# Rolling a matrix along its rows: 512 of 8192 rows taken through SBUF whole

## The chip, the cores and the metric

One Trainium2 chip, one core. The time is device microseconds (us) of one execution, less is better. MB are millions of bytes, GB/s billions of bytes a second.

## The reference

```python
def setup_inputs():
    return {
        "x": np.random.randn(8192, 8192).astype(np.float32),
        "shift": 100,
    }

def reference(x: np.ndarray, shift: int) -> np.ndarray:
    return np.roll(x, shift, axis=1)
```

Each row of 8192 float32 values (32,768 bytes) is rotated by 100 places: `out[r, 100:]` is `x[r, :8092]`, and `out[r, :100]` is `x[r, 8092:]`. Nothing is computed; the kernel only moves 268.44 MB from one place in HBM (the chip's main memory) to another.

## The kernel before

With a shift `s` of 100, the kernel sets `a` to 256 and `g = a - s` to 156. Every output row is cut at column 256.

**The bodies, columns 256 to 8191, are copied from HBM to HBM** (L33 to L43). A block is 64 rows, and each block is four transfers of 16 rows that lie four rows apart; each of the 16 DMA engines gets one row, 7,936 values or 31,744 bytes, of each transfer. The engines SP and ACT issue them in turn, each on its own DMA queue. The last 4 of the 128 blocks have their columns split in two, so that the last transfers are half as long. Each queue issues 248 whole and 16 half transfers and waits for nothing but room in its queue.

**The heads, columns 0 to 255, go through SBUF** (L55 to L80; the core's on-chip memory of 128 partitions), and GpSimd (POOL) issues all their transfers, on a third queue, its ring. They are cut in 16 stages of 512 rows, four rows to a partition (`Q = 4`). A stage has three loads: L72 loads 256 values that straddle a row's end and the next row's start into `t`, for three of the four rows; L73 loads the last 100 values of the fourth row into `h`; L76 loads the first 156 values of the first row into `h`. VectorE (DVE) copies the two parts of `t` to their places in `h` (L74, L77). L80 stores `h`, 256 values for each of 512 rows. The pools `reads` and `heads` have 16 buffers each, one for every stage, so no load waits for a store. In program order GpSimd issues all 48 loads and then the 16 stores. The program uses eight semaphores in turn for GpSimd's transfers, so each transfer is issued only when the one eight places before it has landed.

`single_packet=True` on the heads' transfers asks for few packets. A DMA engine serves its queues by packets, and the trace records each packet with its queue, its bytes, its start and its duration; every transfer also ends with a packet of 4 bytes on each engine that tells its completion.

Of the kernel before, what the change touches and what calls it, by code (L numbers as in the profile page):

```python
# [1 line left out]

# [4 lines left out]


@with_exitstack
def kernel(  # L10
    ctx: ExitStack,
    tc: tile.TileContext,
    x: bass.AP,
    shift: int,
    out: bass.AP,
):
    nc = tc.nc
    n_rows, n_cols = x.shape
    s = shift % n_cols
    a = -(-s // 128) * 128  # L20
    if 0 < a <= 384 and a + 128 <= n_cols:
        a += 128
    g = a - s
    P = nc.NUM_PARTITIONS
    engines = [nc.sync, nc.scalar]
    n_chunks = 16
    rows = n_rows // n_chunks

    xm = x.rearrange("(c e j) w -> c j e w", e=16, j=4)
    om = out.rearrange("(c e j) w -> c j e w", e=16, j=4)
    if a < n_cols:
        blocks = n_rows // 64
        mid = (a + n_cols) // 256 * 128
        for c in range(blocks):
            parts = ((a, mid), (mid, n_cols)) if c >= blocks - 4 and a < mid else ((a, n_cols),)  # L40
            for j in range(4):
                for lo, hi in parts:
                    engines[j % 2].dma_start(out=om[c, j, :, lo:hi], in_=xm[c, j, :, lo - s:hi - s])  # L43
    if a == 0:
        return


    if a > 512:
        for i in range(n_chunks):
            r = slice(i * rows, (i + 1) * rows)  # L50
            nc.gpsimd.dma_start(out=out[r, :s], in_=x[r, n_cols - s:])
            if g > 0:
                nc.gpsimd.dma_start(out=out[r, s:a], in_=x[r, :g])
        return

    Q = 4  # L60
    n_st = n_rows // (P * Q)
    reads = ctx.enter_context(tc.tile_pool(name="reads", bufs=n_st))
    heads = ctx.enter_context(tc.tile_pool(name="heads", bufs=n_st))
    xt = x.rearrange("(k p q) c -> k p q c", q=Q, p=P)
    ot = out.rearrange("(k p q) c -> k p q c", q=Q, p=P)
    tiles = []
    for k in range(n_st):
        t = reads.tile([P, Q - 1, a], x.dtype)
        h = heads.tile([P, Q, a], x.dtype)
        lead = bass.AP(tensor=x.tensor, offset=(k * P * Q + 1) * n_cols - s,  # L70
                       ap=[[Q * n_cols, P], [n_cols, Q - 1], [1, a]])
        nc.gpsimd.dma_start(out=t[:], in_=lead, single_packet=True)  # L72
        nc.gpsimd.dma_start(out=h[:, Q - 1, :s], in_=xt[k, :, Q - 1, n_cols - s:], single_packet=True)  # L73
        nc.vector.tensor_copy(h[:, :Q - 1, :s], t[:, :, :s])  # L74
        if g > 0:
            nc.gpsimd.dma_start(out=h[:, 0, s:], in_=xt[k, :, 0, :g], single_packet=True)  # L76
            nc.vector.tensor_copy(h[:, 1:, s:], t[:, :, s:])  # L77
        tiles.append(h)
    for k, h in enumerate(tiles):
        nc.gpsimd.dma_start(out=ot[k, :, :, :a], in_=h[:], single_packet=True)  # L80


# [1 line left out]
_INS = ['x', 'shift']  # L84
_OUTS = [((8192, 8192), 'float32')]

_NUMBERS = {'shift': 100}


# [26 lines left out]
```

## Time and profile before

| | before |
|---|---|
| median of 3 runs | 817.16 us (816.68 to 817.69) |
| span of the profiled execution | 813.9 us |
| bytes that the DMA engines moved | 276.90 MB, mean 340 GB/s |
| DVE busy | 12.0 us (1% of the span), 32 copies |
| POOL busy (issuing) | 41.1 us (5%) |
| last issue of GpSimd | at 403.4 us |
| issue to landing, 496 KB copy of SP or ACT | 12.5 us |
| issue to landing, head store of 512 KB | 102.9 us |

The profiled execution is a run of its own beside the three; the page gives its span from the first to the last instruction, and no other time of it.

How to read it: the page divides the span in 40 equal slices, and in each it gives the busy share of the DMA engines in tenths and the GB/s that they moved. A queue's line has its packets, its MB, and the time that its packets took as a share of the time of all 16 engines. The queue q0 is GpSimd's ring, q1 and q10 are the queues of SP and ACT. The DMA view gives the same lines for any stretch of the span. A byte that an HBM to HBM copy moves is counted once in an engine's GB/s, though it is read from HBM and written to HBM. The chain of work that ended last is of little use here: it follows GpSimd's ring, whose last issue is in the middle of the span.

### The profile page before, as it was taken

The numbers are of one execution on the slowest core, as the hardware profiler recorded it, in microseconds if no ns is written. First come the engines' busy times: TensorE is split into PE (matmuls) and PEld (weight loads), VectorE is DVE, ScalarE is ACT, GpSimd is POOL, SyncE is SP. The second block draws the span as 40 slices with busy tenths as digits, with TensorE's granted clock in tenths as the row PEclk, the third lists the DMA queues.
The fourth block names the chain that finished last, engine by engine and source line by source line (L and its number), as shares of the span: only waits on it lengthen the run. The fifth ranks groups of instructions, "written<-read, shape, count | busy, mean of one in ns | idle before, by whom it ended". The sixth has DMA issues, their size and how long they took to land. (4 is left out here: it accounts for less than half of the span.)

```text
span 813.9 us, 689 instructions
## 1 busy us (share of the span) xinstructions
DVE 12.0 (1%) x32; POOL 41.1 (5%) x68
## 2 busy tenths in 40 slices
DVE  0000000000000000000000000000000000000000
POOL 2000011111000100000000000000000000000000
DMA  9999999999999999999999999999999999999998
GB/s 314 346 340 344 353 346 350 344 351 344 346 355 346 345 362 354 353 357 354 355 355 349 342 335 331 335 332 325 335 328 332 334 337 334 332 337 332 334 314 293
DMA packets 22277, 276.90 MB, mean 340 GB/s; under 512 B 9472, under 2 KB 9728, under 8 KB 13824
## 3 DMA queue, kind: packets, MB, share of 16 engines
q1 hardware_dynamic: 8448, 130.04, 45.9%
q10 hardware_dynamic: 8448, 130.04, 44.3%
q0 software_dynamic: 5376, 16.78, 8.9%
q14 instruction: 5, 0.04, 0.0%
HBM read 268.44 MB, written 268.44 MB: 660 GB/s over the span
## 5 line engine op out<-in xcount | busy, mean ns | idle before, releaser
L80 POOL DMA_DIRECT2D out_dram<-h x16 | 11.4, 713 | 139.5 <-DMA out_dram<-h 92.5
L76 POOL DMA_DIRECT2D h<-in_x_dram x16 | 8.6, 540 | 158.4 <-DMA t<-in_x_dram 158.4
L72 POOL DMA_DIRECT2D t<-in_x_dram x16 | 12.2, 760 | 32.1 <-DMA h<-in_x_dram 31.3
L73 POOL DMA_DIRECT2D h<-in_x_dram x16 | 8.9, 558 | 32.7 <-DMA h<-in_x_dram 32.7
L74 DVE COPY h<-t 128x300 f32<-128x300 f32 x16 | 5.9, 367 | 268.4 <-DMA t<-in_x_dram 268.4
L77 DVE COPY h<-t 128x468 f32<-128x468 f32 x16 | 7.5, 468 | 0.0
L97 POOL MEMSET const-float32-0.0<- 128x1 f32 x1 | 0.1, 98 | 0.2 <-issue 0.2
L97 POOL MEMSET const-bfloat16-1.0<- 128x1 bf16 x1 | 0.1, 101 | 0.0
L97 POOL MEMSET const-float32-1.0<- 128x1 f32 x1 | 0.1, 98 | 0.0
L97 POOL MEMSET const-uint8-127<- 128x1 uint8 x1 | 0.1, 98 | 0.0
## 6 DMA issues: line engine op xcount, KB each, us to landing
out_dram<-in_x_dram ACTq DMA_DIRECT2D x248, 496.0 KB, 12.5
out_dram<-in_x_dram SPq DMA_DIRECT2D x248, 496.0 KB, 12.5
out_dram<-h POOLq DMA_DIRECT2D x16, 512.0 KB, 102.9
t<-in_x_dram POOLq DMA_DIRECT2D x16, 384.0 KB, 48.9
out_dram<-in_x_dram SPq DMA_DIRECT2D x16, 248.0 KB, 5.9
out_dram<-in_x_dram ACTq DMA_DIRECT2D x16, 248.0 KB, 5.9
h<-in_x_dram POOLq DMA_DIRECT2D x16, 78.0 KB, 41.9
h<-in_x_dram POOLq DMA_DIRECT2D x16, 50.0 KB, 47.2
```

What stands on the lines that cost most here:

```text
L72: nc.gpsimd.dma_start(out=t[:], in_=lead, single_packet=True)
L73: nc.gpsimd.dma_start(out=h[:, Q - 1, :s], in_=xt[k, :, Q - 1, n_cols - s:], single_packet=True)
L74: nc.vector.tensor_copy(h[:, :Q - 1, :s], t[:, :, :s])
L76: nc.gpsimd.dma_start(out=h[:, 0, s:], in_=xt[k, :, 0, :g], single_packet=True)
L77: nc.vector.tensor_copy(h[:, 1:, s:], t[:, :, s:])
L80: nc.gpsimd.dma_start(out=ot[k, :, :, :a], in_=h[:], single_packet=True)
L97: nc = _bacc.Bacc("TRN2", target_bir_lowering=False, num_devices=1)
```

## The change

The last 512 rows are taken out of both parts of the kernel. SP and ACT copy the bodies of 7,680 rows (120 blocks, 232 whole and 16 half transfers for each queue), and there are 15 stages of heads.

The 512 rows go through SBUF whole, as four tiles `w` of 128 rows, a row to a partition. GpSimd loads them before all else: for each tile 8,092 values of each row to their shifted place and the row's last 100 values to its start. After the loads of the ninth stage of heads it issues the four stores of whole tiles, 4,096 KB each.

The pools `reads` and `heads` have 9 buffers instead of 16. So from the ninth stage on a stage's loads are followed by a store of the stage eight before it (`k - depth + 1`), and the buffer that this store frees is used by the next stage. In GpSimd's program the order is: 8 loads of `w`; 27 loads of heads; 4 stores of `w`; the store of stage 0; then for the six stages that are left loads and stores mixed, where the first load into an `h` has to wait until the store of that buffer has landed; then the stores that are left. The transfers of `w` don't ask for `single_packet`.

```diff
+    through = 512 if 0 < a <= 512 and n_rows > 512 and n_cols <= 8192 else 0
     if a < n_cols:
-        blocks = n_rows // 64
+        blocks = (n_rows - through) // 64
...
-    n_st = n_rows // (P * Q)
-    reads = ctx.enter_context(tc.tile_pool(name="reads", bufs=n_st))
-    heads = ctx.enter_context(tc.tile_pool(name="heads", bufs=n_st))
+    n_st = (n_rows - through) // (P * Q)
+    depth = min(n_st, 9 if through else n_st)
+    reads = ctx.enter_context(tc.tile_pool(name="reads", bufs=depth))
+    heads = ctx.enter_context(tc.tile_pool(name="heads", bufs=depth))
+    whole = []
+    if through:
+        rows_in = ctx.enter_context(tc.tile_pool(name="rows_in", bufs=through // P))
+        for i in range(through // P):
+            r = slice(n_rows - through + i * P, n_rows - through + (i + 1) * P)
+            w = rows_in.tile([P, n_cols], x.dtype)
+            nc.gpsimd.dma_start(out=w[:, s:], in_=x[r, :n_cols - s])
+            nc.gpsimd.dma_start(out=w[:, :s], in_=x[r, n_cols - s:])
+            whole.append((r, w))
...
-    for k, h in enumerate(tiles):
-        nc.gpsimd.dma_start(out=ot[k, :, :, :a], in_=h[:], single_packet=True)
+        if k == depth - 1:
+            for r, w in whole:
+                nc.gpsimd.dma_start(out=out[r, :], in_=w[:])
+        if k >= depth - 1:
+            nc.gpsimd.dma_start(out=ot[k - depth + 1, :, :, :a], in_=tiles[k - depth + 1][:], single_packet=True)
+    for k in range(n_st - depth + 1, n_st):
+        nc.gpsimd.dma_start(out=ot[k, :, :, :a], in_=tiles[k][:], single_packet=True)
```

## The prediction

> **What bounds the kernel now.** I read the page's slices first, then its queues, then the queues of three stretches. The slices say that nothing computes and that the DMA engines are always occupied, so the only question is what the transfers wait for.
>
> ```profile
> DMA  9999999999999999999999999999999999999998
> GB/s 314 346 340 344 353 346 350 344 351 344 346 355 346 345 362 354 353 357 354 355 355 349 342 335 331 335 332 325 335 328 332 334 337 334 332 337 332 334 314 293
> ...
> q1 hardware_dynamic: 8448, 130.04, 45.9%
> q10 hardware_dynamic: 8448, 130.04, 44.3%
> q0 software_dynamic: 5376, 16.78, 8.9%
> ...
> HBM read 268.44 MB, written 268.44 MB: 660 GB/s over the span
> ```
>
> q1 and q10 are the queues of SP and ACT and copy HBM to HBM; q0 is GpSimd's ring and moves the head columns through SBUF. A byte of q1 or q10 passes an engine once but is read from and written to HBM; a byte of q0 touches HBM once. So "busy" does not say whether engine or memory is the limit, and the fall of the GB/s row in its second half, where q0 has nothing left, is the hint. Three stretches of 100 us in the DMA view, by queue (packets, MB, share of 16 engines): first heads being loaded (100 to 200 us), then heads being stored (300 to 400), then SP and ACT alone (500 to 600).
>
> ```profile
> q1 hardware_dynamic: 987, 15.68, 41.5%
> q10 hardware_dynamic: 987, 15.68, 39.5%
> q0 software_dynamic: 1284, 3.51, 19.0%
> ```
>
> ```profile
> q1 hardware_dynamic: 978, 15.52, 46.0%
> q10 hardware_dynamic: 980, 15.59, 42.2%
> q0 software_dynamic: 1181, 4.30, 12.4%
> ```
>
> ```profile
> q10 hardware_dynamic: 1042, 16.51, 50.8%
> q1 hardware_dynamic: 1044, 16.57, 49.1%
> q0 software_dynamic: 5, 0.02, 0.0%
> ```
>
> HBM traffic (copies twice, q0 once): 2 x 31.36 + 3.51 = 66.2 MB, 2 x 31.11 + 4.30 = 66.5 MB, 2 x 33.08 + 0.02 = 66.2 MB per 100 us. Three mixes, one rate, 662 to 665 GB/s; I use 664. The engines' own rate differs (349, 354, 331 GB/s), so HBM traffic is what bounds. The engines have a ceiling too: in the trace's packet records the fastest packets of 31,744 B take 1,174 ns, 27.0 B/ns, 433 GB/s for 16 engines. In the load stretch the median copy packet is at that ceiling (1,175 ns), with SP and ACT alone it is 1,473 ns.
>
> **The change, part by part.** HBM traffic stays the same: every element is read once and written once, 536.9 MB. Where HBM stays the limit, nothing changes. The change can cost only where its big transfers make the engines the limit, or where GpSimd's ring ends after the copies.
>
> *Share of the ring.* In the load stretch q0 gets 1,284 packets beside 1,974 of the two copy queues, half of which are 4-byte completions: 1,284 per 987 copy packets with data, 1.30. In the store stretch it is 1,181 per 979, 1.21. Big or small, q0 gets about 1.2 packets per copy packet. So far these are 4 KB (rows of 1 KB, four to a packet). A row of a w tile is 32,368 B on both sides, contiguous; a copy's row of 31,744 B goes as one packet. I assume a w row does too.
>
> *Loading w* (4 tiles). Per engine and tile: 8 rows, a completion, the 8 pieces of 400 B in one packet (as h's 3,200 B are recorded, 126 ns), a completion: 11 packets, 44 in all. At 1.2 they stand beside 36.7 copy packets. HBM traffic of that stage: 16.78 + 2 x 36.7 x 16 x 31,744 B = 54.0 MB, 81.4 us at 664 GB/s. Engine time at the ceiling: 32 x 1.205 + 4 x 0.126 + 36.7 x 1.175 = 82.2 us. So engines and HBM are both at their limit, and the stage costs at least 0.8 us more than its bytes did.
>
> *Storing w.* 9 packets a tile, 36 in all, beside 30 copy packets: 16.78 + 30.5 = 47.3 MB, 71.2 us by HBM; engine time 32 x 1.22 + 30 x 1.175 = 74.3 us, 3.1 us over.
>
> The lower end is thus +3.9 us. The upper end takes the paces of today's stretches, where HBM still slows packets. Load: copies ran at 31.36 MB in 81.0% of 100 us, 387 GB/s, 1.312 us a packet, 1.117 times the ceiling; w alike: 32 x 1.345 + 0.5 + 36.7 x 1.312 = 91.7 us, +10.3. Store: copies 31.11 MB in 88.2%, 1.440 us a packet; q0 4.30 MB in 12.4%, 347 GB/s, 1.512 us for 32 KB: 91.6 us, +20.4. Together +30.7. But at those paces HBM would carry 589 and 516 GB/s, well under 664, so much of the reason for slow packets is gone. The nearest row is the load stretch, and I take half of its slowdown for both stages (copies 1.24 us, w rows 1.27 and 1.285): 86.6 us, +5.2, and 78.3 us, +7.1. Sum **+12.3 us**.
>
> *Fewer copies, one head stage less.* SP and ACT each issue 16 copies of 496 KB fewer, q0 one stage of heads; their HBM bytes are those that w carries, already in the sum. Two copies on DVE and a stage's issues on GpSimd go: 0, beside transfers of 800 us. The last split copies are unchanged, so the end looks as before.
>
> *Reordering on GpSimd.* In program order: 8 w loads, 9 head stages of loads, 4 w stores, then 6 times a head store beside a stage of loads, then 9 stores. Two waits are new. The first head loads wait for w loads (eight transfers in flight at once). With 9 buffers instead of 16, the loads of h in stages 10 to 15 wait until the store that frees the buffer has landed, and behind them on GpSimd stand the later loads and stores. Only q0 waits for these. Its end: 87 + 9 x 15.9 (16 stages took 254 us) + 78 + 6 x (15.9 + 12.2) + 9 x 12.2 (512 KB at 4.30 MB per 100 us) = 587 us, against about 490 now (q0's share is 1.0% in 480 to 500 us). If each of the six stages ran its four transfers one by one at 12 us, 6 x 48 in place of 6 x 28 us, it would end at 706. The copies end near 826, so this is free, below the time of about 120 us more at which it would not be.
>
> Sum: span 813.9 + 12.3 = 826.2. The three times shown have a median of 817.16, 3.3 over the profiled execution's span; of that execution itself only the span is given. So **829.5 us**.
>
> **Rivals.**
> *HBM bound throughout.* If q0 got fewer than about 0.85 of its packets per copy packet, the engines would stay under their ceiling: no change, 817. Against: 1.2 and 1.3. Chance 0.12.
>
> *Faster: HBM carries more when reads, then writes, lead.* It decides where q0's share is low enough that engines do not bind. With w a third of the engine bytes, copies are 33.6 MB and a stage 83.9 MB; the ceiling of 433 GB/s allows 433 x 1.67 = 722 GB/s. Halfway from 664, 693, a stage saves 5.3 us, both 10.6: 806.6. For: in the w stages one direction leads by more than in any stretch of today. Against: the load and store stretches, 5 to 6% leaning either way, carry 662 and 665, SP and ACT alone 662. Chance 0.16. The Trainium skill, "HBM Reference", Specifications (TRN2), gives 716 GB/s for the domain; by it the same stages would save 9.2 us each, 799 us; the trace shows no more than 665 in any of the three stretches.
>
> *w rows go in 4 KB packets.* Then q0 keeps its 35 (load) and 43 GB/s (store): w takes 478 and 390 us. The copies (243.9 MB) would end near 487.7/(664 - 40 GB/s) = 780 us, with q0 some 160 us into storing w; the rest, about 155 packets of w, 6 head stages of 21 and 9 stores of 9, at 0.16 us each and six landings of some 5 us, is 90 us: 870. For: every q0 packet now is about 4 KB. Against: the copies' rows go whole. Chance 0.07. The Trainium skill, "DMA: Bandwidth & Descriptors", SWDGE vs HWDGE vs iDMA, prefers packets of at most 4096 B; q0's packets so far agree, but no row longer than that is in them.
>
> *Engines bind already.* Engine bytes go from 276.9 to 293.1 MB; at the mean of 340 GB/s that is +48 us, 865. For: the DMA row of nines. Against: the copy packets' median of 1,175 ns beside 1,473. Chance 0.05.
>
> *The change doesn't separate loads from stores*, because the ring overtakes: excluded, the w stores stand 27 issues behind the w loads, and those at most eight transfers deep.
>
> **The numbers.** Forecast 0.60, HBM throughout 0.12, faster 0.16, 4 KB packets 0.07, engines 0.05. About 0.2% (1.6 us) is what a measurement of this kernel tells from no change: faster 0.16, same 0.12, slower 0.72. Range 813 to 842: it cuts off half the faster case, the two slow rivals and the last 6 us of the upper end.
>
> **What would show it.** In the changed profile: q0 packets of about 32 KB in two stretches of 80 to 90 us, the first from the start, the second near 230 us; there q0 holds about half of the engines' time, engine GB/s rises to 400 or more, and the HBM traffic worked out as above falls to 600 to 630 GB/s; everywhere else it stays at 662 to 666. q0 ends at 550 to 700 us, before the copies. The forecast is wrong if the w stretches carry 664 or more (then no change or faster), if w takes several hundred us (4 KB packets), or if q0 is last.

## The result, and the profile after

| | before | after |
|---|---|---|
| median of 6 runs | 817.61 us (816.68 to 818.10) | 820.24 us (819.34 to 822.36) |
| ratio to before, 95% interval | | 1.0037 [1.0025, 1.0050] |
| span of the profiled execution | 813.9 us | 817.6 us |
| bytes that the DMA engines moved | 276.90 MB | 293.15 MB |

The changed kernel is slower by 2.6 us by the medians, and by 3.0 us by the ratio. The forecast was 829.5, slower by 12.3: the direction came, at about a fifth of the size.

A profiled run of the changed kernel took 819.34 us with a span of 817.6, so 1.7 us lie outside the span. By that, the profiled execution of the kernel before took about 815.7, less than any of the runs in the table. Differences between two traces of 1 to 2 us are therefore no evidence by themselves; the ratios of the timed runs are.

The page of the changed kernel, the slices of the DMA engines and the queues (packets, MB, share of 16 engines):

```profile
DMA  9999999999999999999999999999999999999998
GB/s 368 405 416 408 423 340 340 358 338 360 339 419 425 429 431 381 348 343 358 338 344 359 345 338 367 364 350 357 351 327 335 332 328 333 337 332 329 336 308 304
...
q1 hardware_dynamic: 7936, 121.91, 41.2%
q10 hardware_dynamic: 7936, 121.91, 40.2%
q0 software_dynamic: 6320, 49.29, 17.9%
...
HBM read 268.44 MB, written 268.44 MB: 657 GB/s over the span
```

The two stretches in which `w` is loaded and stored stand out in the GB/s row: slices 2 to 5 and 12 to 15, over 400 where nearly all of the rest lies between 327 and 368. The engines move 6% more bytes in nearly the same time, because HBM still carries the same 536.9 MB. The records hold 512 packets of 32,368 B and 512 of 32,768 B on q0, so a row of `w` is one packet.

The two stretches in the DMA view, 20 to 90 us (loads of `w`) and 240 to 300 us (stores):

```profile
q0 software_dynamic: 524, 12.45, 43.8%
q10 hardware_dynamic: 526, 8.22, 28.6%
q1 hardware_dynamic: 531, 8.38, 28.4%
```

```profile
q0 software_dynamic: 442, 12.34, 47.8%
q1 hardware_dynamic: 431, 6.83, 26.7%
q10 hardware_dynamic: 426, 6.67, 26.1%
```

The kernel before, 20 to 90 us:

```profile
q1 hardware_dynamic: 695, 11.02, 41.0%
q10 hardware_dynamic: 694, 10.98, 39.7%
q0 software_dynamic: 813, 2.20, 19.2%
```

Two things are to be seen. First the ring's turn: the three queues get nearly the same number of packets, completions counted (524, 526 and 531). Half of a copy queue's packets are completions, so q0 gets 524 packets per 528 copy packets with data, 0.99, and 442 per 428, 1.03; the prediction had taken 1.2. Second the HBM traffic, copies twice and q0 once: 2 x 16.60 + 12.45 = 45.65 MB in 70 us, 652 GB/s, against 660 in the same stretch of the kernel before (24.20 MB moved, 2.20 of them by q0). The forecast was 600 to 630. Over the whole of each stretch, 5 to 96 and 224 to 326 us, the packet records give 645 and 657, and those of the kernel before 659 and 666: by these two traces the stretches fall behind by 1.9 and 1.4 us. Elsewhere, where 662 to 666 was forecast, the changed kernel carries 654 from 120 to 220 us, 663 from 320 to 480 and 663 from 600 to 780.

On GpSimd, the new wait is long, and nobody but the ring waits for it. Three lines of the timeline (start, duration, and in brackets the idle time before): the second head store, the load that waits for the first one to land, and the last issue.

```profile
248.56 0.78 POOL L94 DMA_DIRECT2D out_dram<-h  x1
343.73 0.56 POOL L84 DMA_DIRECT2D h<-in_x_dram  x1 [94.39 <-DMA out_dram<-h]
...
530.77 0.71 POOL L96 DMA_DIRECT2D out_dram<-h  x1 [14.19 <-DMA out_dram<-h]
```

The store stood in the ring behind 16.8 MB of `w`, hence 94 us. The ring's last packet ends near 643 us, 170 us before the copies.

### The profile page after: what moved, and what is told of

Read it like the earlier page. It is cut to its first block, busy times and chain, and to the rows that moved or that the text cites. A ratio compares the mean times of both kernels' runs of the same rounds, so it can differ in the third digit from the quotient of the medians.

```text
span 817.6 us, 670 instructions
## 1 busy us (share of the span) xinstructions
DVE 11.3 (1%) x30; POOL 45.5 (6%) x76
## 2 busy tenths in 40 slices
DMA packets 22197, 293.15 MB, mean 359 GB/s; under 512 B 9088, under 2 KB 9328, under 8 KB 13232
## 4 chain that ended last, share of the span: by engine, by line
another core or an unknown queue 34%; DMA 26%; POOL 2%; issue 2%; POOLq 0%; PEldq 0%
DMA out_dram<-h 12%; DMA t<-in_x_dram 6%; DMA h<-in_x_dram 5%; DMA w<-in_x_dram 3%; POOL h L84 1%; POOL t L83 1%; POOL h L87 1%; POOL out_dram L94 0%; POOLq L127 0%; POOL w L72 0%; POOLq L84 0%; POOLq L94 0%; PEldq L127 0%; POOLq L96 0%
## 5 line engine op out<-in xcount | busy, mean ns | idle before, releaser
L92 POOL DMA_DIRECT2D out_dram<-w x4 | 2.1, 536 | 16.9 <-DMA t<-in_x_dram 10.4
L72 POOL DMA_DIRECT2D w<-in_x_dram x4 | 2.4, 594 | 0.8 <-PEq L127 0.8
L73 POOL DMA_DIRECT2D w<-in_x_dram x4 | 2.3, 565 | 0.0
```

The costliest lines, as they stand in the source:

```text
L72: nc.gpsimd.dma_start(out=w[:, s:], in_=x[r, :n_cols - s])
L73: nc.gpsimd.dma_start(out=w[:, :s], in_=x[r, n_cols - s:])
L92: nc.gpsimd.dma_start(out=out[r, :], in_=w[:])
```

## The experiments

Theory A: the loss sits in the two stretches of `w`, where the packets of 32 KB give the ring so large a share of the engines that these, at their ceiling, no longer bring enough copies to fill HBM. Its rivals: B, the 9 buffers and the loads that wait for stores; and, formed when doubling `w` doubled the loss, C, a price of moving whole rows through SBUF, whatever the share. Each ratio is against the kernel before on the same chip and in the same batch. In the batch of the first four the kernel before takes 826.94 us, in that of the next four 817.24, in that of the last three 818.20. The first and the last batch have the same chip number, so what made the first one slower by 1% is open. So ratios are compared, not times.

| run | ratio to before, 95% interval |
|---|---|
| changed kernel | 1.0037 [1.0025, 1.0050] |
| e1, buffers and order alone | 1.0004 [0.9995, 1.0013] |
| e2, `w` without reuse of buffers | 1.0033 [1.0021, 1.0045] |
| e3, `w` in 16 KB pieces | 1.0024 [1.0013, 1.0035] |
| e4, 1024 rows | 1.0076 [1.0053, 1.0099] |
| e5, halved copies beside the loads of `w` | 1.0102 [1.0084, 1.0121] |
| e6, halved copies without `w` | 1.0003 [0.9986, 1.0020] |
| e7, `w` loaded later | 1.0033 [1.0020, 1.0047] |
| e9, changed kernel again | 1.0036 [1.0021, 1.0052] |
| e10, 16 KB pieces, loaded later | 1.0019 [1.0006, 1.0032] |
| e11, the same, stores in 8 KB pieces | 1.0018 [1.0004, 1.0032] |

**e1: the buffers and the order alone.**

```diff
-    through = 512 if 0 < a <= 512 and n_rows > 512 and n_cols <= 8192 else 0
+    through = 0
-    depth = min(n_st, 9 if through else n_st)
+    depth = 9
```

> No row goes through SBUF whole; all 16 stages of heads are kept, with 9 buffers and the changed order of loads and stores. Theory A (the loss of 2.6 us sits in the two stretches of w, where big packets on GpSimd's ring bring the engines to their ceiling): no change, 817.6 within 0.8. Theory B (the loss comes from the loads that wait for stores and from loads and stores being mixed in the middle of the span): about 820, with HBM traffic under 664 GB/s in the middle stretch.

826.91 us, no change. GpSimd's loads waited 217 us in all for head stores to land, and it cost nothing here. That speaks against B; the next run leaves these waits out beside `w`.

**e2: `w`, and no buffer of heads used twice.**

```diff
-    depth = min(n_st, 9 if through else n_st)
-    reads = ctx.enter_context(tc.tile_pool(name="reads", bufs=depth))
-    heads = ctx.enter_context(tc.tile_pool(name="heads", bufs=depth))
+    depth = n_st
+    reads = ctx.enter_context(tc.tile_pool(name="reads", bufs=4))
+    heads = ctx.enter_context(tc.tile_pool(name="heads", bufs=n_st))
```

> The four w tiles as in the changed kernel, but every stage of heads has its own h buffer (t has 4), so all head loads come before the w stores and no load waits for a store. Theory A: as the changed kernel, 820.2. Theory B: as before, 817.6.

829.48 us, 1.0033: without any such wait the loss stays, with `w`, as A says. B is out.

**e3: rows of `w` in two pieces.**

```diff
-            nc.gpsimd.dma_start(out=w[:, s:], in_=x[r, :n_cols - s])
+            nc.gpsimd.dma_start(out=w[:, s:], in_=x[r, :n_cols - s], max_dma_last_dim=16384)
...
-                nc.gpsimd.dma_start(out=out[r, :], in_=w[:])
+                nc.gpsimd.dma_start(out=out[r, :], in_=w[:], max_dma_last_dim=16384)
```

> The rows of w go in two pieces of 16 KB each, and if the pieces are packets of their own, GpSimd's ring gets about a third of the engine bytes in the stretches of w instead of nearly half. Theory A: copies lead again, HBM is the limit at 664 GB/s, the loss goes, 817.6. Theory B: unchanged, 820.2. The rival that HBM carries more when one direction leads: below 817, since the engines then have room for up to 720 GB/s.

828.64 us, 1.0024, between the two answers; its interval reaches up to e2's 1.0033. The pieces are packets of their own (1,024 of 16,184 B and 1,024 of 16,384 B). The stretch of 20 to 130 us, in which `w` is loaded; then the same stretch of e1, without `w`, in the same batch:

```profile
q10 hardware_dynamic: 924, 14.57, 34.6%
q1 hardware_dynamic: 929, 14.73, 34.2%
q0 software_dynamic: 934, 12.94, 31.6%
```

```profile
q1 hardware_dynamic: 1074, 17.05, 41.2%
q10 hardware_dynamic: 1068, 16.86, 38.9%
q0 software_dynamic: 1349, 3.61, 19.7%
```

With a third of the engine bytes on the ring, HBM carries 2 x 29.30 + 12.94 = 71.5 MB in 110 us, 650 GB/s; without `w`, 2 x 33.91 + 3.61 = 71.4 MB, 649. In this stretch the deficit is gone, as A says; the time of the whole kernel is not back. HBM does not carry more than without `w` either, though reads lead by 42.2 to 29.3 MB: the faster rival of the prediction had its room here and took none of it.

**e4: 1024 rows, in two turns.**

```diff
-    through = 512 if 0 < a <= 512 and n_rows > 512 and n_cols <= 8192 else 0
+    through = 1024 if 0 < a <= 512 and n_rows > 512 and n_cols <= 8192 else 0
...
+        if k == depth + 1:
+            load_whole(4)
+    for r, w in whole[4:]:
+        nc.gpsimd.dma_start(out=out[r, :], in_=w[:])
```

> 1024 rows go through SBUF whole, in two turns of four tiles (loads at the start, stores after nine stages of heads, loads again two stages later, stores after the last head loads); 14 stages of heads. Theory A: twice the stretches of w, twice the loss, 822 to 823. Theory B: four middle stages instead of six, about 819 to 820.

832.15 us, 1.0076: twice the stretches, twice the loss. In the slices of its page four stretches over 400 GB/s stand where the changed kernel has two:

```profile
GB/s 364 408 408 408 411 338 347 335 350 341 347 376 428 429 426 386 349 339 369 417 417 417 414 350 339 360 333 415 426 430 427 346 354 353 350 349 324 326 315 286
```

A and C both allow this. The next two runs tell them apart.

**e5 and e6: the copies beside `w` cut in half,** in the changed kernel (e5) and, as a control, in the kernel before (e6).

```diff
-            parts = ((a, mid), (mid, n_cols)) if c >= blocks - 4 and a < mid else ((a, n_cols),)
+            parts = ((a, mid), (mid, n_cols)) if (c < 10 or c >= blocks - 4) and a < mid else ((a, n_cols),)
```

> The changed kernel, with the copies of the first 10 blocks cut in two (packets of 15,872 B), so that GpSimd's ring holds about 0.61 of the engine bytes while w is loaded, instead of 0.44. Theory A (engines at their ceiling): at the pace of 415 GB/s that the engines showed there, HBM traffic falls to about 575 GB/s in that stretch, some 6 us more than the changed kernel: ratio to before about 1.011. Theory C (whole rows through the ring have a price of their own, whatever the share): no more than the changed kernel and the control's own cost, 1.003 to 1.005.

> The kernel before, with the copies of the first 10 blocks cut in two. The control for the run with halved copies beside w: both theories expect about no change, since HBM stays the limit, up to 1 us if half copies can't keep the queues full.

e5 took 825.74 us, 1.0102, where A had named 1.011; e6 817.52, 1.0003. The stretch of 20 to 70 us of e5, then of e6:

```profile
q0 software_dynamic: 554, 12.63, 59.0%
q1 hardware_dynamic: 553, 4.38, 20.8%
q10 hardware_dynamic: 551, 4.35, 20.6%
```

```profile
q0 software_dynamic: 1940, 5.30, 34.5%
q1 hardware_dynamic: 858, 6.79, 34.1%
q10 hardware_dynamic: 854, 6.73, 32.9%
```

In e5 the engines move 427 GB/s, but three fifths of it are the ring's, and HBM carries 2 x 8.73 + 12.63 = 30.1 MB in 50 us, 602 GB/s (A had named 575). In e6 they move less, 377 GB/s, and HBM carries 2 x 13.52 + 5.30 = 32.3 MB, 647. The same cut of the copies costs nothing that shows without `w`, and with it about 5.3 us (1.0102 against the changed kernel's 1.0037). The share of the ring makes that, not the rows as such: A. C, a price that the share doesn't change, can't be the cause of these 5.3 us; a smaller price of that kind beside A is not ruled out by it.

**e7: `w` loaded behind the fourth stage of heads.** The lines that load `w` move into the loop; where they are taken out isn't shown.

```diff
     for k in range(n_st):
+        if k == 4:
+            for i in range(through // P):
+                r = slice(n_rows - through + i * P, n_rows - through + (i + 1) * P)
+                w = rows_in.tile([P, n_cols], x.dtype)
+                nc.gpsimd.dma_start(out=w[:, s:], in_=x[r, :n_cols - s])
+                nc.gpsimd.dma_start(out=w[:, :s], in_=x[r, n_cols - s:])
+                whole.append((r, w))
```

> The changed kernel, with the loads of w behind the loads of the fourth stage of heads instead of ahead of the first. If the first 20 us, where HBM carried 614 GB/s with w and 642 without, are a cost of their own: about 0.8 us less, 1.0025 to 1.003. Theory A otherwise: as the changed kernel, 1.0037. Theory C: the same 1.0037.

819.89 us, 1.0033 with an interval of 1.0020 to 1.0047, which holds both answers. That the start costs 0.8 us is not shown by it. (From 5 to 20 us the packet records give 622 GB/s with `w` and 650 without.)

**e8: the ring alone.**

```diff
-    if a < n_cols:
+    if False:
         blocks = (n_rows - through) // 64
```

> SP and ACT issue no copies, so columns 256 to 8191 of the first 7,680 rows are left out of the output; GpSimd's part is as in the changed kernel. Theory A: nothing competes, and the loads and stores of w run at the engines' ceiling of 433 GB/s, packets of 32 KB at 1.20 and 1.21 us, about 39 us for each set of four tiles, with HBM traffic at 433 GB/s too, far below 664. If w's packets stay at 1.27 us alone, they have a price of their own (theory C).

The stretch of 8 to 38 us, in which `w` is loaded:

```profile
DMA packets 543, 13.07 MB, mean 436 GB/s; under 512 B 96, under 2 KB 96, under 8 KB 144
...
q0 software_dynamic: 543, 13.07, 101.7%
```

A packet counts whole where it starts, so the share is over 100%; scaled back to 100%, the 436 GB/s are 429. That is within 1% of the 433 that the prediction took for a ceiling, here with HBM traffic of no more than that, far from the 660 that HBM carries elsewhere. So the limit is in the engines, and the loads of `w` reach it (mean packet of loads and stores 1.23 us; 1.20 and 1.21 were expected; each set of four tiles takes 40 us, 39 expected). Alone, the packets of `w` show no price of their own. The Trainium skill, "DMA: Bandwidth & Descriptors", Specifications, gives 435 GB/s for the fabric; this run comes within 2% of it.

**e9, e10, e11: less of the ring at a time.** e9 is the changed kernel once more. e10 joins the edits of e3 and e7; e11 changes one number of e10:

```diff
-                nc.gpsimd.dma_start(out=out[r, :], in_=w[:], max_dma_last_dim=16384)
+                nc.gpsimd.dma_start(out=out[r, :], in_=w[:], max_dma_last_dim=8192)
```

> The changed kernel once more, to stand beside the next two on one chip: 1.0025 to 1.005 times before.

> w in pieces of 16 KB as before, and its loads behind the fourth stage of heads. Theory A: GpSimd's ring holds about 0.31 of the engine bytes beside w, HBM is the limit all along, and the start is that of the kernel before: 1.000 to 1.001. If the 1.0024 of the earlier run with 16 KB pieces has another reason than the ceiling and the start: 1.002 again.

> As the run before it, with the stores of w in pieces of 8 KB (the loads stay at 16 KB). Theory A: the ring holds about 0.2 of the engine bytes beside the stores, further from the ceiling, 1.000 to 1.001; the ring ends at about 800 us, beside the last copies, where engines have stood idle for 9 to 22% of the time, so it may gain there, not below 0.997. If the time depends on how long the ring is busy rather than on its share: above 1.002.

820.85, 819.31 and 819.00 us beside 818.20. Smaller pieces about halve the loss, 1.0036 to 1.0019 and 1.0018. The intervals against the kernel before overlap, but the twelve runs of e9 have a mean of 821.1 us, and those of e10 and e11 819.4 and 819.2, with a standard error of 0.6 us on the difference. In the stretches of `w` no clear deficit is left; the stores of `w` in e11, 310 to 450 us:

```profile
q1 hardware_dynamic: 1282, 20.32, 41.0%
q10 hardware_dynamic: 1283, 20.35, 36.7%
q0 software_dynamic: 1502, 11.72, 22.9%
```

2 x 40.67 + 11.72 = 93.1 MB in 140 us are 665 GB/s, what the kernel before carries. A expected 1.000 to 1.001. So about 0.002, some 1.5 us by the ratios (1.1 and 0.8 by the medians), is left that the ceiling does not explain and no experiment places. It is about half of the changed kernel's loss. A price of rows through SBUF at any share, theory C at half its size, would fit it and was not tested. It does not grow with the time that the ring is busy: in e11 the ring works until about 807 us, in e10 until 735, with the same ratio. The end of the kernel did not gain from a ring still at work there. No version beats the kernel before.

## Why the prediction was right or wrong

**HBM traffic bounds the kernel, and the change leaves it as it is: right.** 16 MB more through the engines cost 2.6 us and not the 48 that their bytes would at 340 GB/s; stretches with 0, 10, 22 and 31% of the engine bytes on the ring carry HBM traffic within 1% of each other (662 and 662 in the kernel before, 665 in e11; 650 in e3, beside 649 at 10% in e1 of the same batch). An exception is e6, where 28% beside half copies carried 647, 2% less than the 660 of the kernel before in that stretch, at no loss for the whole.

**The loss is in the stretches of `w`, where the engines come to their ceiling: right as a mechanism, shown for about half of the loss.** e2 and e4 tie the loss to `w`, e5 against e6 shows that the ring's share costs, e8 shows the ceiling. In e10 and e11, where the share is small, about half of the loss goes; the other half is open.

**The ring's share, 1.2 packets per copy packet: mis-sized, the first of the two steps that failed.** With rows of 32 KB it is 0.99 and 1.03. The ratio was read off 4 KB packets and carried over to packets eight times as long. e6 shows that it is no constant at all: 1,940 per 856, 2.3, of the same small packets beside half copies. At 1.0, 44 copy packets stand beside the loads and 36 beside the stores, so more HBM bytes are carried in the stretch, and the time that HBM needs for them comes closer to the time that the engines need.

**The pace, half of today's slowdown: mis-sized, the second step that failed.** Copies were to take 1.24 us a packet, and took 1.21 beside the loads and 1.225 beside the stores, 82% and 74% of them within 6 ns of 1.175 (54% and 27% in the same stretches of the kernel before). `w` was to take 1.27 and 1.285, and took 1.27 and 1.223. The stretch's own floor was the nearer row: where HBM carries less than it can, most packets run at the floor, and the slowdown of stretches in which HBM is full says little of them.

With the prediction's 1.2 and these packets the sum is 36.7 x 1.21 + 32 x 1.27 + 0.5 - 81.4 = 4.1 for the loads and 30 x 1.225 + 32 x 1.223 - 71.2 = 4.7 for the stores, 8.8 in place of 12.3. With 1.0 as well it is 94.4 - 92.6 = 1.8 and 83.2 - 80.4 = 2.8, together 4.6 (61.5 and 53.4 MB at 664). So, of the 9.7 that the forecast was too high, the pace accounts for 3.5 us and the share for 4.2; taken in the other order, 3.9 and 3.8. Neither was the smaller fault. The last 2.0 are not placed: the sum puts packet times end to end against a flat 664, and the two traces, good to 1 or 2 us, put the loss of the stretches at 1.9 + 1.4 = 3.3.

The two lower terms that the prediction worked out, 0.8 and 3.1, come to 3.9 and were closer than the choice, but that is luck in part. With the share that was measured, the same floor packets need 90.8 us for the loads, less than HBM's 92.6, so nothing would be lost there, and 81.3 against 80.4 for the stores, 0.9. By these floors the engines stop being the limit at 1.13 packets of the ring per copy packet beside the loads and 0.93 beside the stores, and not at 0.85, as the rival of HBM bound throughout has it. That rival was nearer than its chance of 0.12 says. The loads lose time all the same, since both limits lie close together there and packets run above their floor.

**Packets of 32 KB, two stretches, the ring ending before the copies, waits for stores free: right.** The rival with 4 KB packets is out by the records. So is the one with engines that bind already, and the one in which HBM carries more when one direction leads: e3, with reads leading by 42 to 29 MB, stayed at 650 GB/s. The Trainium skill's 716 GB/s ("HBM Reference", Specifications (TRN2)) was reached in no stretch worked out here; the highest is 665. Its preference for packets of at most 4096 B ("DMA: Bandwidth & Descriptors", SWDGE vs HWDGE vs iDMA) does not cut a longer row: 32,768 B went whole. The prediction said that q0's packets until then agree with it; 256 of them in the kernel before have 4,368 B, a little more.

**Left open:** the 1.5 us that remain with small pieces, about half of the loss.

## What to carry to other kernels

Where transfers keep the engines busy all the time, count the traffic of each resource over stretches with a different mix; the one that stays constant is the bound, and here 16 MB more engine bytes were nearly free. A transfer through SBUF touches HBM once per engine byte where a copy touches it twice: it costs when its share of the engine bytes is so large that the ceiling times (2 - share) comes near what HBM carries, or falls under it. Here a share of 0.31 would allow 733 GB/s, and HBM carried its usual 650 (e3); 0.43 would allow 680, and the loads of `w` carried 652, a little under the usual; 0.59 allows 610, and e5 carried 602. So small pieces on that queue are safer than whole rows. For a stretch that leaves a limit, the durations at the new limit are nearer than a part of the slowdown at the old one; where two limits lie close together, expect packets somewhat above the floor.

## What the runs showed of the hardware that was not expected

The ring's turn depends on what stands beside it. In the stretches shown in which `w` moves in rows or pieces of 16 KB and more, the three queues get the same number of packets within 4%, if a completion of 4 B is counted as a packet like any other: 524, 526 and 531 in the changed kernel, 554, 553 and 551 in e5, 934, 929 and 924 in e3. As a copy has one completion to each packet of data on an engine, that is 1.0 packet of the ring per copy packet with data. With 4 KB packets the ring gets more: 1.2 to 1.3 beside copies of 31.7 KB, and 2.3 beside copies of 15.9 KB. In e6 the head loads went at 106 GB/s (5.30 MB in 50 us) instead of 31 (2.20 MB in 70 us before), at no gain and no loss for the whole. Why the turn differs was not tried. A row of 32,768 B goes as one packet on GpSimd's ring, and one transfer's option, `max_dma_last_dim`, cuts it into packets of 16 or 8 KB.
